# A fused decoder layer on one core: early loads, laid-out bias tiles, separate norm and tanh stages, final scaling on ScalarE

## The chip, the cores and the metric

The kernel runs on one core of a Trainium2 chip. The metric is device time in microseconds of one execution. The texts name the engines TensorE (PE in the rows, PEld its weight loads), VectorE (DVE), ScalarE (ACT), GpSimd (POOL) and SyncE (SP, which only issues transfers here).

## The reference, cut to what matters

One layer (`DEPTH` 1) of a decoder trunk on 512 tokens and 1024 channels, all in float32:

```python
h = rmsnorm(x, norm_mix_g)
proj = h @ w_in                     # mLSTM q,k,v,o,i,f | attention q,k,v | two gates
# branch A: mLSTM, 4 heads x 128: causal conv (width 4) and SiLU on q and k,
#   exponential input gate, sigmoid forget gate, running-max stabiliser
hm = head_rmsnorm(num / max(|den|, exp(-m)), m_norm_g);  ya = (sigmoid(o) * hm) @ w_br_m
# branch B: differential attention, 4 heads, q/k 2 x 64, v 128, causal
a = softmax(q1 k1^T / 8 + bias) - lam * softmax(q2 k2^T / 8 + bias)   # bias: rel_bias[t5_bucket(i - j)]
hd = head_rmsnorm(a @ v, da_norm_g) * (1 - lam_init);  yb = hd @ w_br_d
x = x + (sigmoid(g_a) * ya + sigmoid(g_b) * yb) @ w_out
# FFN: rmsnorm, up (2 x 2816), causal conv (width 3), gelu(gate) * value, down; added to x
x = x + sigmoid(rmsnorm(x) @ w_ple_gate) * (p @ w_ple)
return rmsnorm(x, norm_final_g)
```

## The kernel before, in words

Activations lie with channels on the 128 partitions and 512 tokens along the row, in eight tiles. Each float32 operand of a product is split into a rounded high part (ScalarE, `split`, L89) and the rest (VectorE, L90), and a product is three matmuls: high x high, high x rest, rest x high (`mm3`, L97 to L99). A weight tile of 128x1024 is loaded by SP into `raw` (two buffers), then split into `whi` and `wlo` (two buffers each; `wload`). A projection onto 128 channels is 24 matmuls into one of four PSUM banks of tag `mm`.

The stages: (1) `vproj` for the mLSTM values: eight pairs of an `x` tile and half a weight tile, each pair loaded and split as its buffers come free; squares of `x` are summed for the norm (`rms`). Nine warm matmuls without use run first. (2) The steps of `ORDER`: `if` the scalar gates and their scans (`gates`), `mq`, `mk` conv and SiLU (`conv_silu`), `m` scores and weighted sums of one mLSTM head, `M` its end with norm and output gate, `dq`, `dk`, `dv`, `a`, `A` the same for attention, `ga`, `gb` the branch gates. (3) The merge of the branches, `w_out`, the FFN, and the last part, done in four blocks of 128 tokens, the last of them in halves.

A planner (the tile framework) orders each engine's instructions from the program order as a priority and from its own estimate of times; it also sets all waits. Engines run their queues in order. A tile of a tag waits for a free buffer of the tag; `tc.issue_after` only orders two instructions of one engine, and `tc.high_priority` moves a piece ahead.

The lines of importance: the gate rows are scanned on VectorE (L324, L329), stored to DRAM (`rd`, L332), and each head reads its rows back as a broadcast onto 128 partitions (`rb`, L429), exponentiates (L430), masks (POOL, L431) and multiplies with the scores `s`. The position bias (`make_bias`) is made from a one-hot product on TensorE (`bvp`, L357), stored, broadcast in DRAM and read back with a skew. `rsqrt_of` is a logarithm, an exponential and one Newton step, and loads ScalarE's table with the logarithm ahead (L155); tanh uses another table.

Of the kernel before, what the change touches and what calls it, by code (L numbers as in the profile page):

```python
# [16 lines left out]
P = 128  # L17
# [3 lines left out]
H = 4  # L21
# [16 lines left out]
C_BI = 256  # L38
C_BF = 257
NPAR = 258  # L40
# [10 lines left out]
bias0 if0 mq0 mk0 mq1 mk1 ct0 m0 m1 mk3 mq2 dk0 M0 M1 mk2 m2 mq3 M2 m3 dq0 dv0 M3 a0 dk1 dq1  # L51
A0 a1 A1 dk2 dq2 ga3 dq3 a2 A2 ga0 ga2 gb1 dk3 a3 gb3 gb2 gb0 ga1 A3
# [4 lines left out]
def trunk_kernel(ctx, tc, xT, pT, par, oneh, relb, lamv, w_if, w_in, w_v, w_br, w_out, w_up,  # L57
# [92 lines left out]

    def rsqrt_of(r, v, a, before=None):
# [5 lines left out]
        nc.scalar.activation(r, r, AF.Exp, scale=-0.5, bias=lnb)  # L157
# [23 lines left out]

    ident = cp.tile([P, P], F32, name="ident")
# [16 lines left out]

    def conv_silu(c, scale, name):  # L200
# [3 lines left out]
        nc.gpsimd.memset(u[:, 0:3], 0.0)  # L204
# [13 lines left out]
    def halves(c, name):  # L218

        o = ps("mm", name)  # L220
        proj(o, win(c), 0, h)
        y = tt("ev", "y")
        nc.vector.tensor_mul(y, o, rB)
        return y, (slice(0, 64), slice(64, P))

    def queries(c, name):

        y, rows = halves(c, name)
# [22 lines left out]
    def vw(i, g, kk, old):  # L251

        if old is None:
            raw = wp.tile([P, 1024], F32, tag="raw", name="raw", bufs=2)
            hi = wp.tile([P, 1024], F32R, tag="whi", name="whi", bufs=2)
            lo = wp.tile([P, 1024], F32R, tag="wlo", name="wlo", bufs=2)
            old = (hi, lo, raw)
        hi, lo, raw = old
        c = slice(kk * S, (kk + 1) * S)
        nc.sync.dma_start(raw[:, c], w_v[4 * i + g][:, c])  # L260
        split(hi[:, c], lo[:, c], raw[:, c])
        return old

    def vproj(i, name, first=None):
        os = [ps("mm", f"{name}p{b}") for b in range(NB)]
        xs = []
        for g in range(4):
            w = None if first else wload(w_v[4 * i + g])
            for kk in range(2):
                k = 2 * g + kk  # L270
                if first:
                    x = tt("x", f"x{k}")
                    nc.sync.dma_start(x, xT[:, k, :])
                    h.append(scaled(x, C_GMIX + k, f"h{k}"))
                    w = vw(i, g, kk, w)
                    if k == 1:
                        nc.sync.dma_start(prm[:, KD:], par[:, KD:])
                    xs.append(x)
# [18 lines left out]
    def gates():  # L297
# [3 lines left out]
        with tc.high_priority(offset=180):  # L301
            nc.sync.dma_start(raw, w_if)
# [8 lines left out]
        gi, gf = tt("hn", "gi")[0:H, :], tt("rb", "gf")[0:H, :]  # L311
        for t, c, a in ((gi, C_BI, 0), (gf, C_BF, 32)):
            nc.vector.scalar_tensor_tensor(t, gt[a:a + H, :], prm[a:a + H, c:c + 1], g2[a:a + H, :],
                                           op0=ALU.add, op1=ALU.add)
        e = tt("rb", "ge")[0:H, :]
# [31 lines left out]
    def make_bias():  # L347
        tab = cp.tile([REL_BUCKETS + 1, H], F32, name="tab")
        nc.vector.memset(tab, NEG)
        nc.gpsimd.dma_start(tab[0:REL_BUCKETS, :], relb)  # L350
        bvd = dp.tile([H, 640], F32, name="bvd")
        for i in range(2):
            half = slice(i * 320, (i + 1) * 320)
            oh = tt("hn", "oh", 320)[0:REL_BUCKETS + 1, :]
            nc.gpsimd.dma_start(oh, oneh[:, half])
            o = ps("acc", "bvp", 320)
            nc.tensor.matmul(o[0:H, :], lhsT=tab, rhs=oh, start=True, stop=True)  # L357
            bv = tt("hn", "bv", 320)[0:H, :]
            nc.scalar.activation(bv, o[0:H, :], AF.Copy, scale=8.0)
            nc.gpsimd.dma_start(bvd[:, half], bv)  # L360
        rows = dp.tile([P, H * 640], F32, name="bvrows")
        nc.gpsimd.dma_start(rows, bvd.rearrange("h u -> (h u)").partition_broadcast(P))
        bias = []
        for hh in range(H):
            t = f(rt("bt", f"bias{hh}"))
            src = bass.AP(tensor=rows.tensor, offset=rows[0, hh * 640 + P - 1:hh * 640 + P].offset,
                          ap=[[H * 640 - 1, P], [1, S]])
            nc.gpsimd.dma_start(t, src)
            bias.append(t)
        return bias  # L370
# [36 lines left out]
    def head_norm(o, g, name, extra=None):  # L407

        y = tt("hn", "y")
        nc.scalar.activation(y, o, AF.Copy, scale=col(g))  # L410
        v = tt("hn", "v")
        nc.scalar.activation(v, o, AF.Square)
        ss = ps("sc", name + "ss")
        last = colsum(ss, v)
        if extra is None:
            nc.vector.tensor_scalar(v, ss, 1.0 / P, EPS, op0=ALU.mult, op1=ALU.add)
        else:
            nc.vector.scalar_tensor_tensor(v, ss, 1.0 / P, extra, op0=ALU.mult, op1=ALU.add)
        r = tt("hn", "r")
        rsqrt_of(r, v, ss, last)  # L420
        nc.vector.tensor_mul(y, y, r)
        return y
# [24 lines left out]
    def mlstm_end(hh, num, den, t):  # L447
        em = tt("rb", "em")
# [6 lines left out]
        y = head_norm(num, C_GM + hh, f"hm{hh}", em)  # L455
# [8 lines left out]
    def attention(hh, q, k):  # L464
        av = []
        for i in range(NB):
# [3 lines left out]
            for z in range(2):  # L470
                s = ps("sc", f"ds{hh}{i}{z}", nw)
                for b in range(2):
# [5 lines left out]
                    out=e, in0=s[:, :n], in1=bias[hh][:, S - n:], scale=0.125, scalar=-3.0e38,  # L478
# [17 lines left out]
    def attention_end(hh, o):  # L496
        y = head_norm(o, C_GD + hh, f"hd{hh}")
# [4 lines left out]
    def gate(c, name):  # L502
# [4 lines left out]
        nc.scalar.activation(t, t, AF.Tanh, scale=0.5)  # L507
# [5 lines left out]
    for step in ORDER.split():  # L513
# [13 lines left out]
        elif what == "M":  # L527
            hm[i] = mlstm_end(i, *sums[i], mo.get(i))
        elif what == "dv":
# [322 lines left out]
```

## Time and profile before

| | |
|---|---|
| time, median of 3 runs | 830.45 us (830.2 to 831.01) |
| the profiled execution | 831.68 us; its span 830.0 us |
| TensorE busy | 813.1 us (98%), 3665 matmuls |
| TensorE weight loads | 666.0 us (80%) |
| VectorE / ScalarE / GpSimd busy | 541.2 (65%) / 412.5 (50%) / 28.9 us (3%) |
| HBM traffic over the span | 104 GB/s |

Busy time is the union of an engine's instructions; matmuls overlap their successors, so a busy TensorE isn't one at its peak. An engine's idle time costs something only where TensorE, or the chain to the last output, waits for it.

### The profile page before, as it was taken

The page shows a single profiled execution, that of the slowest core. Times are in us where ns is not written, and L with a number is a line of the kernel's source. Part 1 is how long each engine was busy: PE and PEld are TensorE (multiplying, and loading weights), DVE is VectorE, ACT ScalarE, POOL GpSimd, SP SyncE. Part 2 cuts the span into 40 slices and gives each one's busy share as a digit, 9 for nine tenths or more (in the row PEclk, how much of TensorE's full clock was granted, in tenths as well). Part 3 has the DMA queues.
Part 4 walks back from the last instruction along what each step waited for, and adds up shares of the span by engine and source line. Part 5 has one row for each costly group of instructions (what it writes and reads, how often), then busy time and mean ns, then how long its engine had stood idle before and what let it go on. Part 6 is the DMA issues. An engine that isn't in the chain of part 4 may idle for free.

```text
span 830.0 us, 9910 instructions
## 1 busy us (share of the span) xinstructions
PE 813.1 (98%) x3665; PEld 666.0 (80%) x3665; DVE 541.2 (65%) x875; ACT 412.5 (50%) x624; POOL 28.9 (3%) x117
## 2 busy tenths in 40 slices
PE   9999999999999999999999999999999999999995
PEld 7777778887878888888788888888888888888884
DVE  7698787699767854456677777777777343343546
ACT  7556877687776433234654444444444432232433
POOL 0111100000000000000000000000000000000000
PEclk9999999999999999999999999999999999999998
DMA  6472333222122233352333222333223323333402
GB/s 223 136 207 96 102 109 109 78 77 71 58 76 77 77 102 102 123 181 92 111 103 102 101 82 97 102 108 120 87 92 101 96 89 99 94 112 96 142 36 77
DMA packets 28425, 85.97 MB, mean 104 GB/s; under 512 B 3462, under 2 KB 5146, under 8 KB 28248
## 3 DMA queue, kind: packets, MB, share of 16 engines
q1 hardware_dynamic: 27256, 81.96, 30.9%
q0 software_dynamic: 832, 3.11, 1.3%
q8 instruction: 29, 0.48, 0.2%
q10 hardware_dynamic: 288, 0.27, 0.1%
q14 instruction: 20, 0.16, 0.1%
HBM read 83.19 MB, written 3.45 MB: 104 GB/s over the span
## 4 chain that ended last, share of the span: by engine, by line
PE 85%; ACT 5%; DMA 4%; DVE 4%; issue 1%; POOL 0%; SPq 0%; POOLq 0%; DVEq 0%; ACTq 0%
PE uv L99 5%; PE wd L98 5%; PE wd L99 5%; PE uv L97 5%; PE uv L98 5%; PE wd L97 5%; PE ug L99 5%; PE ug L97 5%; PE ug L98 5%; PE gb L98 2%; PE gb L97 2%; PE gb L99 2%; PE ga L97 2%; PE ga L99 2%; PE ga L98 2%; PE wo L97 2%
## 5 line engine op out<-in xcount | busy, mean ns | idle before, releaser
L89 ACT CAST whi<-raw 128x1024 fp32r<-128x1024 f32 (+1 forms) x137 | 138.3, 1010 | 206.4 <-issue 73.0
L90 DVE TENSOR_TENSOR wlo<-raw,whi 128x1024 fp32r<-128x1024 f32 (+1 forms) x136 | 159.8, 1176 | 87.2 <-ACT whi L89 85.8
L97 PE MATMUL wd<-gh,whi 128*128 128x512 f32 x176 | 68.5, 389 | 0.0
L98 PE MATMUL wd<-gl,whi 128*128 128x512 f32 x176 | 68.5, 389 | 0.0
L99 PE MATMUL wd<-gh,wlo 128*128 128x512 f32 x176 | 68.5, 389 | 0.0
L588 DVE SCALAR_TENSOR_TENSOR y<-u,prm,y 128x512 f32<-128x512 f32 x88 | 65.6, 749 | 1.5
L89 ACT CAST gh<-y 128x512 fp32r<-128x512 f32 x22 | 13.7, 621 | 55.5 <-DVE y L597 55.5
L583 DVE TENSOR_TENSOR u<-uv,rffn 128x512 f32<-128x512 f32 x22 | 15.2, 692 | 38.2 <-PE uv L99 38.2
L97 PEld LDWEIGHTS wd<-gh,whi 128*128 128x128 f32 x176 | 33.0, 188 | 6.9
L98 PEld LDWEIGHTS wd<-gl,whi 128*128 128x128 f32 x176 | 33.0, 188 | 6.9
L99 PEld LDWEIGHTS wd<-gh,wlo 128*128 128x128 f32 x176 | 33.0, 188 | 6.8
L586 ACT ACTIVATE y<-u,prm 128x512 f32<-128x512 f32 x44 | 35.7, 814 | 0.2
L595 ACT ACTIVATE y<-y 128x512 f32<-128x512 f32 x22 | 13.9, 632 | 38.9 <-DVE y L588 38.9
L97 PE MATMUL wo<-mxh,whi 128*128 128x512 f32 x64 | 24.9, 389 | 0.0
L98 PE MATMUL wo<-mxl,whi 128*128 128x512 f32 x64 | 24.9, 389 | 0.0
L99 PE MATMUL wo<-mxh,wlo 128*128 128x512 f32 x64 | 24.9, 389 | 0.0
L90 DVE TENSOR_TENSOR gl<-y,gh 128x512 fp32r<-128x512 f32 x22 | 15.2, 692 | 14.7 <-ACT gh L89 14.7
L481 ACT ACTIVATE e<-e,mx 128x128 f32<-128x128 f32 (+3 forms) x32 | 17.8, 558 | 7.0 <-DVE mx L480 6.8
L210 DVE SCALAR_TENSOR_TENSOR y<-u,prm,y 128x512 f32<-128x512 f32 x24 | 17.8, 743 | 2.1 <-ACT y L208 2.0
L582 POOL MEMSET u<- 128x2 f32 x44 | 4.3, 99 | 366.6 <-DVE y L588 357.2
L571 DVE TENSOR_TENSOR x<-x,wo 128x512 f32<-128x512 f32 x8 | 5.5, 687 | 17.2 <-PE wo L99 17.2
L477 DVE CUSTOM_DVE_ANT_0 e<-ds,bias 128x128 f32<-128x128 f32 (+3 forms) x32 | 15.1, 482 | 2.3 <-PE ds L473 2.2
(1093 smaller groups left out, 2226.7 us busy)
## 6 DMA issues: line engine op xcount, KB each, us to landing
raw<-in_w_up SPq DMA_DIRECT2D x44, 512.0 KB, 3.3
raw<-in_w_in SPq DMA_DIRECT2D x36, 512.0 KB, 3.4
raw<-in_w_down SPq DMA_DIRECT2D x16, 512.0 KB, 3.6
x<-in_xT SPq DMA_DIRECT2D x16, 256.0 KB, 4.5
raw<-in_w_br SPq DMA_DIRECT2D x8, 512.0 KB, 3.2
raw<-in_w_out SPq DMA_DIRECT2D x8, 512.0 KB, 3.8
raw<-in_w_gate SPq DMA_DIRECT2D x8, 512.0 KB, 3.4
raw<-in_w_down SPq DMA_DIRECT2D x8, 384.0 KB, 3.3
```

What stands on the lines that cost most here:

```text
L89: nc.scalar.copy(hi, src)
L90: nc.vector.tensor_sub(lo, src, f(hi))
L97: nc.tensor.matmul(o, lhsT=lh, rhs=rh, start=start, stop=False)
L98: nc.tensor.matmul(o, lhsT=lh, rhs=rl, start=False, stop=False)
L99: nc.tensor.matmul(o, lhsT=ll, rhs=rh, start=False, stop=stop)
L210: nc.vector.scalar_tensor_tensor(y, u[:, i:i + S], col(c0 + i), y, op0=ALU.mult, op1=ALU.add)
L477: nc.vector.tensor_tensor_reduce(out=e, in0=s[:, :n], in1=bias[hh][:, S - n:], scale=0.125, scalar=-3.0e38, op0=ALU.add, op1=ALU.max, accu ...
L481: nc.scalar.activation(e, e, AF.Exp, bias=mx[:, 1:2], accum_out=mx[:, 2:3])
L583: nc.vector.tensor_mul(u[:, 2:514], o, rB)
L586: nc.scalar.activation(y, u[:, 2:514], AF.Identity, scale=col(c0 + 2), bias=col(c0 + 3))
L588: nc.vector.scalar_tensor_tensor(y, u[:, i:i + S], col(c0 + i), y, op0=ALU.mult, op1=ALU.add)
L595: nc.scalar.activation(gt, gt, AF.Gelu_apprx_tanh)
```

## The change

- The eight `x` tiles and the eight weight halves of the first stage are all issued on SP at the start, the halves into buffers of tag `hz` in place of `raw`; the other parameters follow, and the load for `if` behind them. The first half of `whi` is copied on VectorE.
- The position bias comes as four tiles laid out beforehand, loaded by POOL, at a later step (`bias0` behind `mk2`), behind the last `memset` traced up to there. The factor 1/8 moves from the softmax's reduction to the queries.
- The scalar gates add their biases in one instruction of 36 rows in place of two of 4 rows.
- `M` ends with the product of gate and numerator and with the mean square; the rest of the norm and the split are steps `N` of their own, behind the first attention head and later. Only head 0 of the attention loads the logarithm's table ahead.
- The tanh of the branch gates are issued behind the last exponential of the attention norms, in the merge loop.
- In the last part the product with the final gain comes ahead of the norm, and the scaling by the norm is on ScalarE for the first three blocks; the last block's halves are multiplied first, then finished with priority.

```diff
-bias0 if0 mq0 mk0 mq1 mk1 ct0 m0 m1 mk3 mq2 dk0 M0 M1 mk2 m2 mq3 M2 m3 dq0 dv0 M3 a0 dk1 dq1
-A0 a1 A1 dk2 dq2 ga3 dq3 a2 A2 ga0 ga2 gb1 dk3 a3 gb3 gb2 gb0 ga1 A3
+if0 mq0 mk0 mq1 mk1 ct0 m0 m1 mk3 mq2 dk0 M0 M1 mk2 bias0 m2 mq3 M2 m3 dq0 dv0 M3 a0 dk1 dq1
+A0 a1 N0 A1 dk2 dq2 N1 ga3 dq3 a2 N2 A2 ga0 ga2 gb1 dk3 N3 a3 gb3 gb2 gb0 ga1 A3
...
+    for k in range(KD):
+        xs.append(tt("x", f"x{k}"))
+        nc.sync.dma_start(xs[k], xT[:, k, :])
+        raws.append(f(rt("hz", f"raw{k}")))
+        nc.sync.dma_start(raws[k], w_v[k // 2][:, k % 2 * S:(k % 2 + 1) * S])
+    fed = nc.sync.dma_start(prm[:, KD:], par[:, KD:])
...
+        if g + kk == 0:
+            nc.vector.tensor_copy(hi[:, c], raw)
+            nc.vector.tensor_sub(lo[:, c], raw, f(hi[:, c]))
+        else:
+            split(hi[:, c], lo[:, c], raw)
...
+        nc.vector.scalar_tensor_tensor(g2[0:36, :], gt[0:36, :], prm[0:36, C_B:C_B + 1], g2[0:36, :],
+                                       op0=ALU.add, op1=ALU.add)
+        gi, gf = g2[0:H, :], g2[32:32 + H, :]
...
     def make_bias():
...
+            with tc.issue_after(last_pool.ins):
+                nc.gpsimd.dma_start(t, biasT[:, hh * S:(hh + 1) * S])
...
     def mlstm_end(hh, num, den, t):
...
+        y, v = f(rt("hz", f"hmy{hh}")), f(rt("hz", f"hmv{hh}"))
+        nc.scalar.activation(y, num, AF.Copy, scale=col(C_GM + hh))
+        ss, _ = mean_square(num, v, f"hm{hh}")
+        nc.vector.scalar_tensor_tensor(v, ss, 1.0 / P, em, op0=ALU.mult, op1=ALU.add)
...
+        return y, v
+
+    def mlstm_norm(hh, y, v):
+        r, t = tt("hn", "r"), tt("hn", "t")
+        rsqrt_of(r, v, t)
+        nc.vector.tensor_mul(t, y, r)
         hi, lo = rt("hz", f"hmh{hh}"), rt("hz", f"hml{hh}")
-        split(hi, lo, y, 0.5)
+        split(hi, lo, t, 0.5)
...
+        rsqrt_of(r, v, ss, None if hh else last)
...
-        nc.scalar.activation(t, t, AF.Tanh, scale=0.5)
         return t
...
+        with tc.issue_after(last_exp.ins):
+            for t in (ta, tb):
+                nc.scalar.activation(t, t, AF.Tanh, scale=0.5)
...
         for n in range(2):
-            x = x3[b, n]
-            nc.vector.scalar_tensor_tensor(x, x, r, gB[n], op0=ALU.mult, op1=ALU.mult)
-            nc.sync.dma_start(out[b][:, n * S:(n + 1) * S], x)
+            nc.scalar.activation(x3[b, n], x3[b, n], AF.Copy, scale=r)
+            nc.sync.dma_start(out[b][:, n * S:(n + 1) * S], x3[b, n])
...
+        nc.vector.tensor_scalar_mul(x[:, :half], x[:, :half], r)
+        nc.vector.scalar_tensor_tensor(x[:, half:], x[:, half:], r, gB[1][:, half:], op0=ALU.mult, op1=ALU.mult)
         nc.sync.dma_start(out[b][:, S:], x)
...
+        nc.scalar.activation(x3[b, 0], x3[b, 0], AF.Copy, scale=r)
+        nc.scalar.dma_start(out[b][:, :S], x3[b, 0])
...
+        with tc.high_priority():
+            x = embed(b, S, half, os[0], xt[:, :half], 1)
+            nc.vector.tensor_scalar(ss[b][:, 3:4], ss[b][:, 0:1], ss[b][:, 1:2], D * EPS, op0=ALU.add, op1=ALU.add)
+            embed(b, S + half, half, os[1], xt[:, half:], 2)
+        nc.vector.tensor_mul(x, x, gB[1][:, :half])
```

## Rows read from the trace of the kernel before

**Rows 1.** Waits of TensorE: engine, line, waited for: us in total, times, longest.
```profile
PE num L97 <- ACT pph L89: 2.5, 4, 1.4
PE s L97 <- ACT mk0h L92: 2.0, 1, 2.0
```

**Rows 2.** By stretches: length, busy us of each engine, granted clock, DMA share, GB/s.
```profile
62.00:160.00 98.00, 94.30 (x433) 76.74 (x434) 75.54 (x118) 71.78 (x116) 8.59 (x31) 0.98 0.32 100
160.00:280.00 120.00, 119.70 (x566) 96.09 (x566) 97.32 (x254) 87.50 (x165) 3.67 (x15) 1.00 0.22 71
```

**Rows 3.** Timeline of the head: start, us, engine, line, operation, out<-in, count, idle before.
```profile
1.52 4.21 PE L126 MATMUL warm<-idle 128*128 128x512 f32 x9 [1.52 <-DVE idle L123]
...
4.32 0.72 ACT L139 ACTIVATE h0h<-x,prm 128x512 fp32r<-128x512 f32 x1 [1.79 <-DMA prm<-in_par]
...
5.07 0.75 DVE L140 SCALAR_TENSOR_TENSOR h0l<-x,prm,h0h 128x512 fp32r<-128x512 f32 x1 [3.19 <-ACT h0h L139]
...
5.46 0.60 ACT L89 CAST whi<-raw 128x512 fp32r<-128x512 f32 x1
...
6.12 0.50 PE L97 MATMUL mvp<-whi,h0h 128*128 128x512 f32 x1 [0.39 <-ACT whi L89]
```

**Rows 4.** Timeline of TensorE around the first bias product.
```profile
29.16 0.40 PE L99 MATMUL mvp<-whi,h7l 128*128 128x512 f32 x1
29.49 0.70 PE L357 MATMUL bvp<-oh,tab 33*4 33x320 f32 x2
30.12 0.50 PE L307 MATMUL if<-h0h,whi 128*128 128x512 f32 x1
```

**Rows 5.** Timeline of VectorE behind the gate matmuls.
```profile
36.30 0.28 DVE L377 TENSOR_TENSOR lvp<-lv 128x128 f32<-128x128 f32 x1
...
38.20 0.14 DVE L383 TENSOR_TENSOR nlam<-lexp 128x1 f32<-128x1 f32 x1
38.37 0.74 DVE L313 SCALAR_TENSOR_TENSOR gf<-gt,prm,g 4x512 f32<-4x512 f32 x1
```

**Rows 6.** Chain of waits, 40 to 63 us: start, us, what.
```profile
49.48 3.00 DMA rd<-rows
...
62.87 0.50 PE s L97
```

**Rows 7.** By stretches, granted clock third from the end.
```profile
63.60:67.10 3.50, 3.50 (x10) 2.92 (x10) 3.50 (x6) 0.62 (x1) 0.10 (x1) 0.51 0.00 0
87.00:89.00 2.00, 0.72 (x4) 0.26 (x2) 0.76 (x2) 1.62 (x5) 0.29 (x1) 1.00 0.71 109
```

**Rows 8.** Table loads of ScalarE: groups of 60 to 300 us, and timeline at 91.
```profile
L155 ACT ACT_TABLE_LOAD x8 | 10.3, 1283 | 0.1
...
L507 ACT ACT_TABLE_LOAD x4 | 5.1, 1283 | 0.1
...
91.74 1.28 ACT L155 ACT_TABLE_LOAD   x1
93.03 0.64 ACT L450 ACTIVATE em<-em 128x512 f32<-128x512 f32 x1
```

**Rows 9.** A norm's step on VectorE by line; the last softmax by stretches.
```profile
L159 DVE SCALAR_TENSOR_TENSOR hm0ss<-v,hm0ss x1: 689/689/689, 104.6 to 104.6; 128x512 f32<-128x512 f32 x1
...
250.00:260.00 10.00, 10.00 (x50) 8.28 (x49) 9.98 (x38) 8.08 (x19) 0.00 (x0) 1.00 0.33 104
260.00:270.00 10.00, 10.00 (x50) 8.07 (x49) 4.57 (x9) 5.54 (x11) 0.35 (x2) 1.00 0.15 53
```

**Rows 10.** Timeline of the end.
```profile
820.40 0.47 ACT L710 ACTIVATE pg<-pgs,rple 128x256 f32<-128x256 f32 x1 [2.28 <-PE pgs L99]
820.86 0.42 DVE L712 SCALAR_TENSOR_TENSOR pg<-pg,pw 128x256 f32<-128x256 f32 x1
...
822.85 0.41 DVE L716 TENSOR_TENSOR x<-pg,xt 128x256 f32<-128x256 f32 x1
...
823.83 0.43 DVE L769 TENSOR_TENSOR x<-x,gfin 128x256 f32<-128x256 f32 x1 [0.57 <-ACT pg L717]
824.17 0.21 DVE L732 TENSOR_SCALAR v<-ss 128x1 f32<-128x1 f32 x1
...
825.60 0.51 ACT L738 ACTIVATE x<-x,rf 128x256 f32<-128x256 f32 x1 [1.80 <-DVE rf L662]
...
826.44 0.35 ACTq L740 DMA_DIRECT2D out<-x  x1
```

More of the change, by code (lines that the diff above doesn't have):

```diff
@@ L37 @@
 C_FCONV = 80
-C_BI = 256
-C_BF = 257
-NPAR = 258
+C_B = 256
+NPAR = 257
 ROW_OFF = [0, 512, 896, 1152, 1280]
@@ L156, in rsqrt_of @@
         nc.scalar.activation(r, v, AF.Ln, scale=2.0 ** -LN_SHIFT)
-        nc.scalar.activation(r, r, AF.Exp, scale=-0.5, bias=lnb)
+        nonlocal last_exp
+        last_exp = nc.scalar.activation(r, r, AF.Exp, scale=-0.5, bias=lnb)
         nc.scalar.activation(a, r, AF.Square)
@@ L198, in win @@
         return wload(w_in[c])
+    last_pool = None
     def conv_silu(c, scale, name):
@@ L216, in conv_silu, with halves @@
         return hi, lo
-    def halves(c, name):
+    def halves(c, name, scale=1.0):
         o = ps("mm", name)
@@ L222, in halves @@
         y = tt("ev", "y")
-        nc.vector.tensor_mul(y, o, rB)
+        nc.vector.scalar_tensor_tensor(y, o, scale, rB, op0=ALU.mult, op1=ALU.mult)
         return y, (slice(0, 64), slice(64, P))
     def queries(c, name):
-        y, rows = halves(c, name)
+        y, rows = halves(c, name, 0.125)
         qs = []
@@ L249, in keys, with vw @@
         return ks
-    def vw(i, g, kk, old):
+    def vw(g, kk, old):
         if old is None:
-            raw = wp.tile([P, 1024], F32, tag="raw", name="raw", bufs=2)
             hi = wp.tile([P, 1024], F32R, tag="whi", name="whi", bufs=2)
             lo = wp.tile([P, 1024], F32R, tag="wlo", name="wlo", bufs=2)
-            old = (hi, lo, raw)
-        hi, lo, raw = old
+            old = (hi, lo)
+        hi, lo = old
         c = slice(kk * S, (kk + 1) * S)
-        nc.sync.dma_start(raw[:, c], w_v[4 * i + g][:, c])
-        split(hi[:, c], lo[:, c], raw[:, c])
+        raw = raws[2 * g + kk]
+        if g + kk == 0:
[3 more added lines that the diff above has]
+            split(hi[:, c], lo[:, c], raw)
         return old
@@ L301, in gates @@
         with tc.high_priority(offset=180):
-            nc.sync.dma_start(raw, w_if)
+            with tc.issue_after(fed.ins):
+                nc.sync.dma_start(raw, w_if)
             split(w[:, :, 0:64], w[:, :, 64:P], raw.rearrange("p (k c) -> p k c", c=64))
@@ L347, in make_bias @@
     def make_bias():
[L348 to L363, printed above, removed]
+        out = []
         for hh in range(H):
             t = f(rt("bt", f"bias{hh}"))
[L366 to L370, printed above, removed]
+            with tc.issue_after(last_pool.ins):
+                nc.gpsimd.dma_start(t, biasT[:, hh * S:(hh + 1) * S])
+            out.append(t)
+        return out
     def make_nlam():
@@ L405, in weighted, with mean_square @@
             nc.tensor.matmul(o, lhsT=ones, rhs=pl, start=False, stop=j == NB - 1)
[L407 to L411, printed above, removed]
+    def mean_square(o, v, name):
         nc.scalar.activation(v, o, AF.Square)
         ss = ps("sc", name + "ss")
[L414 to L422, printed above, removed]
+        return ss, colsum(ss, v)
     def mlstm(hh):
@@ L477, in attention @@
                 nc.vector.tensor_tensor_reduce(
-                    out=e, in0=s[:, :n], in1=bias[hh][:, S - n:], scale=0.125, scalar=-3.0e38,
+                    out=e, in0=s[:, :n], in1=bias[hh][:, S - n:], scale=1.0, scalar=-3.0e38,
                     op0=ALU.add, op1=ALU.max, accum_out=mx[:, 0:1])
@@ L496, in attention_end @@
     def attention_end(hh, o):
-        y = head_norm(o, C_GD + hh, f"hd{hh}")
+        y, v, r = tt("hn", "y"), tt("hn", "v"), tt("hn", "r")
+        nc.scalar.activation(y, o, AF.Copy, scale=col(C_GD + hh))
+        ss, last = mean_square(o, v, f"hd{hh}")
+        nc.vector.tensor_scalar(v, ss, 1.0 / P, EPS, op0=ALU.mult, op1=ALU.add)
+        rsqrt_of(r, v, ss, None if hh else last)
+        nc.vector.tensor_mul(y, y, r)
         hi, lo = rt("hz", f"hdh{hh}"), rt("hz", f"hdl{hh}")
@@ L528, in trunk_kernel @@
             hm[i] = mlstm_end(i, *sums[i], mo.get(i))
+        elif what == "N":
+            hm[i] = mlstm_norm(i, *hm[i])
         elif what == "dv":
@@ L796, in _bucket_onehot @@
     b = np.where(n < exact, n, np.minimum(large, REL_BUCKETS - 1))
-    b = np.where(u <= 511, b, REL_BUCKETS)
-    return (b[None, :] == np.arange(REL_BUCKETS + 1)[:, None]).astype(np.float32)
+    t = np.concatenate([rel_bias, np.full((1, H), NEG, np.float32)])[np.where(future, REL_BUCKETS, b)]
+    return t.transpose(0, 2, 1).reshape(P, H * S)
 def _pack(x, p, rel_bias, norm_mix_g, w_in, b_if, m_conv_w, m_conv_b, m_norm_g, da_lambda, da_norm_g,
```

67 lines of the change are left out of this document (26 added, 41 removed).

## The prediction, made before the changed kernel was built or run

> **What bounds the kernel now.** I read the page first: its engine line gives TensorE 813.1 of 830.0 us, the other engines 65% at most (both stand in the small table). So an edit pays only where it removes TensorE work, closes a gap in TensorE, or shortens the ends where TensorE doesn't work. The waits of TensorE come next: the gaps are few, the longest single one 2.0 us before the first score matmul of the mLSTM (`s`), which waits for ScalarE's `mk0h`, and four of 2.5 us together before `num` [rows 1]. The view by stretches says where: the mLSTM stage (62 to 160 us) has 98 − 94.30 = 3.7 us without TensorE work, the attention stage (160 to 280) only 0.3 [rows 2]. The timelines of the two ends and of the places that the diff touches give the terms. The profiled execution took 831.68 us, 1.68 more than its span; the median of the runs shown is 830.45, 1.23 less. I sum against 831.68 and subtract 1.23 at the end.
>
> **Head.** The first projection matmul starts at 6.12 us, behind `h0h` (ScalarE, from 4.32), `acc` and then `whi`, the last to come; the warm matmuls keep TensorE busy until 1.52 + 4.21 = 5.73 [rows 3]. The change gives the first half of `whi` to VectorE, which is idle then, so ScalarE's queue no longer stands in the way. `h0h` still waits for the parameter load that ScalarE issues first, which the change leaves alone. Then the warm matmuls end last: 6.12 − 5.73 = 0.4 saved. Bounds: 0.6 saved (they overlap their successor) and 0.4 lost, where VectorE takes the 0.75 us `h0l` ahead of the copy. I take −0.4. That the sixteen loads go out without waiting for the `raw` buffers gives nothing to TensorE here: of its few waits [rows 1] only the first, for `whi`, lies in this stage. The load of the remaining parameters moves behind them; its first reader is beyond 34 us.
>
> **Position bias.** Two matmul groups `bvp` go: TensorE spends 30.12 − 29.49 = 0.63 us on the first, the second repeats it at 34 us [rows 4]. Together −1.26. Nothing hides them, since the projections stand right behind. The bound is half of that: the first pair may have covered the wait of `if` for a free PSUM bank. The four loads of laid-out bias and the five-step chain through DRAM leave POOL's queue at this place; four loads come back behind `mk2`, and the `lamv` load with them. The masks of head 2 can stand behind the five issues in POOL's queue; POOL is busy only 8.59 of 98 us in that stage [rows 2], so it has the time. I take 0; if the cover is gone, a mask is late by what five issues take.
>
> **The wait at 60.5 us.** From the gate matmuls a chain leads over VectorE's scans, a store to DRAM and the broadcast back to ScalarE's `rb`, behind which `mk0h` stands in ScalarE's queue. The change takes from VectorE in this stretch `lvp` and `lsum` (0.28 each), one of two gate additions (0.74) and two small `nlam` steps (0.15 each): 1.6 us [rows 5]. VectorE is the one that sets the pace here, so the chain is 1.6 us shorter, while TensorE arrives 0.63 us earlier (the second `bvp` lies between). The wait becomes 2.02 − 1.6 + 0.63 = 1.05, a gain of 0.97. More may come: the store of `rows` takes 3.00 us there, beside the bias transfers that go [rows 6]. After the wait TensorE's granted clock was 0.51 for 3.5 us, its lower level of 1.2 GHz, which costs 3.5 × 0.49 = 1.7; after a stretch with 0.72 us of work in 2 us it stayed at 1.00 [rows 7]. So with a wait of about 1 us I also count the 1.7 as saved: −2.7 in all. Bounds: −3.7 (all of it) and +2 (the written order of TensorE is made anew by the planner, and a wait as long as this one may appear elsewhere).
>
> **mLSTM and attention.** Tanh and the logarithm sit in different tables. In the stage from 60 to 300 us the two lines with most of the loads have 12, of 1.283 us [rows 8]. With the norms moved behind the first attention head and the gates' tanh behind the last exponential, two are left, so at least 10 × 1.283 = 12.8 us leave ScalarE. Of the norms, per head, a logarithm, an exponential, a square and a split move from the mLSTM to the attention stage on ScalarE; on VectorE four instructions of about 0.69 us (one is shown), 2.8 us per head, 11 us in all [rows 9]. So the mLSTM stage gets easier, where ScalarE was busy 71.78 of 98 us, and VectorE rises from 97.3 to 108 of 120 us in the attention stage. `s` starts at 62.87 [rows 6], so 0.87 of the 3.7 us of the mLSTM stage belong to the wait before it, and 2.8 remain; all name ScalarE [rows 1]. I take −0.5 for both stages; bounds −2.8 and the 11 us of VectorE. At the merge of the branches, the sixteen tanh and one table load stand on ScalarE while TensorE still has the products of the other heads; ScalarE is busy 5.54 of 10 us there [rows 9]: 0. Without that cover it is the load and the first two tanh, some 2.7 us by the rows of `h0h` and of the loads.
> Weighed against the trace: behind a table load at 91.74 the next ScalarE instruction starts at 93.03, 1.29 us later [rows 8]. The Trainium skill (ScalarE: Activation LUTs, section "What ACT_TABLE_LOAD costs") gives 1.28 for the load and 1.38 more for a drain, 2.66 for each switch. By the page the same ten loads would free 27 us of ScalarE; the trace shows no such drain, and as ScalarE isn't what the end waits for, the sum would move by no more than the bound above.
>
> **Tail.** After the last matmul ScalarE's tanh starts at 820.40, but VectorE, held by two scalings of the block before that wait for its norm and by a product with the final gain, reaches the last half's addition only at 822.85 [rows 10]. The change puts block 2's scaling on ScalarE and the gain products ahead, so nothing ahead of the multiply on VectorE waits for the norm any more, and I count it free at 820.5. Then the tanh (0.47) ends at 820.87, the multiply takes 0.42, so the addition starts at 821.3. From there to the scale took 825.60 − 822.85 = 2.75, of which 0.34 is the gain product in front of `v`; 2.41 remain: scale at 823.7. ScalarE's half is now 512 wide; the nearest row of that kind, `h0h`, took 0.72: 824.4, and a little for the issue: 824.6 instead of 826.44, −1.8. Bounds −2.0 and 0 (the two new ScalarE scalings, waiting for POOL's power, stand ahead of the tanh in its queue).
>
> **Sum.** −0.4 − 1.3 − 2.7 − 0.5 − 1.8 = −6.7: 831.68 − 6.7 = 825.0, less 1.23: 823.8 us.
>
> **Rivals.**
> A. The wait before `s` stays. The planner that orders TensorE places `s` where it believes `mk0h` ready, and a chain that it also believes shorter is answered by an earlier `s`. For it: the order was made from planned times, and the chip missed them here by the 2.0 us of [rows 1]. Against it: the transfers of the chain get lighter, which a plan need not see. Then 2.7 is missing: 831.68 − 4.0 − 1.23 = 826.5.
> B. The emptier ScalarE closes the mLSTM stage altogether, and the wait at 60 us goes whole: 1.0 and 2.3 more, 820.5. For it: the waits of [rows 1] for `num` and `s` name ScalarE. Against it: `rb`, which ScalarE works on ahead of them, still comes by DRAM.
> C. Slower: VectorE becomes the bound in the attention stage. It is busy 9.98 of 10 us in the softmax of the last head, with 4.57 of 10 right after [rows 9]; the 11 us of norm work fit only if they fall into the light stretches. VectorE works in order, so a norm that stands ahead of a head's softmax holds all its scores, and TensorE, once the gate projections are used up, waits. Price 2.8 us for each head, 11.2 with all four: 831.68 − 6.2 + 11.2 − 1.23 = 835.5. It decides from 6.2 us on, where it has eaten the other terms, that is from the third head. Against it: 22.7 us of VectorE are free in the stage, and eight gate projections of 24 matmuls each are there to fill.
> D. The new order doesn't do what it says: table loads are put back between logarithm and tanh, as the planner may bring a norm forward. They cost ScalarE 1.283 each and TensorE little; the time is that of the forecast without the 0.5: 824.3, within its own range.
>
> **How the numbers follow.** Forecast with D 0.47, A 0.25, B 0.16, C 0.12. The likeliest gives 823.8, its own range 821.5 to 825.5. For 8 in 10 the range goes down to 819.5 (B, with both ends at their bounds) and up to 830, which takes in A with the head and the first `bvp` unpaid, and the beginning of C. What the measurement can tell apart is about 0.2%, 1.7 us: faster means under 828.8, slower over 832.1. The forecast and B are faster, A but for 0.02 at its upper end; of C two thirds end slower, the rest within. Faster 0.86, same 0.06, slower 0.08.
>
> **What would show it.** Right: first projection matmul at about 5.7; no `bvp`; the first `s` waits 1 us or less and the granted clock stays at 1.00 after it; two table loads from 60 to 300 us; VectorE at 90% from 160 to 280 us with TensorE gaps there under 1 us; last output issue 4.2 us after the last tanh starts, not 826.44 − 820.40 = 6.0. Wrong: a granted clock of 0.5 anywhere after the start, TensorE waiting in the attention stage for VectorE's `mx`, or a tanh of the last block held in ScalarE's queue.

## The result, and the profile after

The changed kernel is slower: median 835.84 us (835.26 to 836.90, 4 runs) beside 830.73 (830.20 to 831.17, 4 runs) of the kernel before on the same chip, ratio 1.0057 [1.0037, 1.0078]. The profiled execution took 836.26 us, its span 833.3.

To see where the time went, I cut the span at four events of TensorE that both kernels have. (In after, `hd2ss` and other steps are reordered, so a landmark inside a stage can mislead; between these four TensorE has the same matmuls in both kernels, but for the four of `bvp`.) The forecast gave its −0.5 to the mLSTM and the attention stage together; it stands in the mLSTM's row here.

| stretch of TensorE, us | before | after | difference | forecast |
|---|---|---|---|---|
| start to last `mvp` (head) | 29.56 | 29.88 | +0.32 | −0.4 |
| last `mvp` to first `ds` (gates, mLSTM) | 135.74 | 129.96 | −5.78 | −4.5 (`bvp` −1.26, wait −2.7, stage −0.5) |
| first `ds` to last `yb` (attention, merge) | 191.91 | 200.68 | +8.77 | 0 |
| last `yb` to last `pgs` (`w_out`, FFN) | 463.10 | 463.06 | −0.04 | 0 |
| last `pgs` to the end (tail) | 9.66 | 9.70 | +0.04 | −1.8 |

The differences add up to 3.3 us, that of the two spans, while the medians lie 5.1 apart. The profiled execution after took 2.96 us outside its span, the one before 1.68: that is 1.3 of the other 1.8, for which no stage accounts.

TensorE's waits after (engine, line, waited for: us in total, times, longest):

```profile
PE yb L96 <- ACT hdh L91: 6.5, 1, 6.5
...
PE s L96 <- ACT mk0h L91: 1.4, 1, 1.4
PE num L96 <- ACT pph L88: 1.1, 2, 0.6
```

`s` and `num` wait less than in [rows 1]; a new wait of 6.5 us is longer than all of those. It stands at the merge of the branches, where the products of the last attention head, `hd3`, are due. The stretches (columns as in [rows 2], the last one lies around the end of the wait):

```profile
62.00:160.00 98.00, 96.90 (x455) 79.44 (x454) 71.14 (x113) 57.72 (x98) 11.50 (x35) 1.00 0.35 116
160.00:280.00 120.00, 113.89 (x539) 90.29 (x537) 100.39 (x260) 82.24 (x166) 3.72 (x15) 0.99 0.19 66
277.84:284.67 6.83, 4.00 (x9) 2.81 (x10) 4.58 (x7) 5.39 (x9) 0.00 (x0) 0.50 0.00 0
```

In the mLSTM stage 98 − 96.90 = 1.1 us are without TensorE work instead of 3.7; in the attention stage 6.1 instead of 0.3. Around the end of the wait TensorE's granted clock is 0.50, its level of 1.2 GHz, for 6.83 us, as it was for some 3.5 us behind the wait at 60 us in the kernel before [rows 7]; there it now stays at 1.00.

What holds `hdh`: ScalarE's timeline at the merge, after.

```profile
273.80 0.72 ACT L159 ACTIVATE r<-r,lnb 128x512 f32<-128x512 f32 x1
274.54 1.28 ACT L555 ACT_TABLE_LOAD   x1
275.84 0.63 ACT L555 ACTIVATE ga<-ga 128x512 f32<-128x512 f32 x1
276.37 0.58 ACT L160 ACTIVATE hd3ss<-r 128x512 f32<-128x512 f32 x1
...
279.49 0.61 ACT L555 ACTIVATE ga<-ga 128x512 f32<-128x512 f32 x1
280.01 0.61 ACT L91 ACTIVATE hdh<-y 128x512 fp32r<-128x512 f32 x1
```

And VectorE's, after:

```profile
276.50 0.69 DVE L560 SCALAR_TENSOR_TENSOR ga<-ga,ya 128x512 f32<-128x512 f32 x1 [3.40 <-ACT ga L555]
277.10 0.69 DVE L161 SCALAR_TENSOR_TENSOR hd3ss<-v,hd3ss 128x512 f32<-128x512 f32 x1
277.83 0.69 DVE L162 SCALAR_TENSOR_TENSOR r<-hd3ss,r 128x512 f32<-128x512 f32 x1
```

The same place before, ScalarE:

```profile
272.94 0.72 ACT L157 ACTIVATE r<-r,lnb 128x512 f32<-128x512 f32 x1
273.69 0.60 ACT L158 ACTIVATE hd3ss<-r 128x512 f32<-128x512 f32 x1
276.51 0.63 ACT L92 ACTIVATE hdh<-y 128x512 fp32r<-128x512 f32 x1 [2.21 <-DVE y L421]
```

From the last exponential to the split `hdh` it took 276.51 − 272.94 = 3.57 us before and 280.01 − 273.80 = 6.21 after: the table load and a tanh stand ahead of the square that the norm needs, more tanh ahead of the split, and VectorE's product `ga` waits 3.40 us for its tanh with the norm's steps queued behind it. That is 2.6 us of the 6.5. The rest is that the last head comes late: TensorE was 5.45 us ahead at the first `ds`, yet its `hd3ss` (the sum of squares for the last head's norm) ends at 272.37 instead of 271.11.

The head after, ScalarE:

```profile
4.79 0.72 ACT L138 ACTIVATE h0h<-x,prm 128x512 fp32r<-128x512 f32 x1 [2.26 <-DMA prm<-in_par]
```

VectorE:

```profile
5.54 0.75 DVE L139 SCALAR_TENSOR_TENSOR h0l<-x,prm,h0h 128x512 fp32r<-128x512 f32 x1 [3.58 <-ACT h0h L138]
6.21 0.42 DVE L275 CAST whi<-raw 128x512 fp32r<-128x512 f32 x1
```

`h0l` does stand ahead of the copy, and `h0h`, which waits for the parameters, starts 0.47 us later than in [rows 3] (over all runs it starts between 4.20 and 5.25); the first `mvp` starts at 6.78 instead of 6.12. From there on TensorE waits for nothing in this stage.

The tail after, ScalarE, VectorE and the last issue:

```profile
823.62 1.32 ACT L730 ACTIVATE x<-x,rf 128x512 f32<-128x512 f32 x2
824.84 0.45 ACT L714 ACTIVATE pg<-pgs,rple 128x256 f32<-128x256 f32 x1
...
825.78 0.42 DVE L720 TENSOR_TENSOR x<-pg,xt 128x256 f32<-128x256 f32 x1
...
828.15 0.72 ACT L739 ACTIVATE x<-x,rf 128x512 f32<-128x512 f32 x1 [1.41 <-DVE rf L666]
828.90 0.38 ACTq L740 DMA_DIRECT2D out<-x  x1
```

From the start of the last tanh to the last issue it is 828.90 − 824.84 = 4.1 us, as forecast, instead of 6.0 [rows 10]. But the two scalings of block 2 stand ahead of that tanh, and it starts 1.26 us behind the last matmul's end (823.58) instead of 0.09. From the last issue to the end of the span it takes 4.4 us instead of 3.5. These two, 1.2 and 0.8, use up the gain of 2.0; the forecast counted on neither. No run was made for the second.

### The profile page after: what moved, and what is told of

The parts are those of the page before. It is cut to its first block, busy times and chain, and to the rows that moved or that the text cites. A ratio compares the mean times of both kernels' runs of the same rounds, so it can differ in the third digit from the quotient of the medians.

```text
span 833.3 us, 9859 instructions
## 1 busy us (share of the span) xinstructions
PE 811.2 (97%) x3661; PEld 665.4 (80%) x3661; DVE 539.7 (65%) x873; ACT 397.8 (48%) x614; POOL 27.3 (3%) x111
## 4 chain that ended last, share of the span: by engine, by line
PE 81%; ACT 2%; issue 1%; DVE 1%; POOL 0%; POOLq 0%; DVEq 0%; ACTq 0%
PE uv L96 5%; PE wd L98 5%; PE wd L96 5%; PE uv L98 5%; PE uv L97 5%; PE wd L97 5%; PE ug L96 5%; PE ug L98 5%; PE ug L97 5%; PE ga L96 2%; PE ga L98 2%; PE ga L97 2%; PE gb L98 2%; PE gb L97 2%; PE gb L96 2%; PE wo L96 2%
## 5 line engine op out<-in xcount | busy, mean ns | idle before, releaser
L89 DVE TENSOR_TENSOR wlo<-raw,whi 128x1024 fp32r<-128x1024 f32 (+2 forms) x135 | 159.3, 1180 | 89.5 <-ACT whi L88 88.1
L96 PE MATMUL yb<-hdh,whi 128*128 128x512 f32 x32 | 13.2, 412 | 6.5 <-ACT hdh L91 6.5
```

What stands on the lines that cost most here:

```text
L89: nc.vector.tensor_sub(lo, src, f(hi))
L96: nc.tensor.matmul(o, lhsT=lh, rhs=rh, start=start, stop=False)
```

## The experiments

Each compares with the kernel before on its own chip. Two theories of the attention stretch's 8.8 us: **T**, the deferred tanh of the gates (table load and tanh in front of the last norm); **N**, the norms that moved from the mLSTM into the attention stage (rival C of the prediction; in the expectations of e13 and e14, C and E are two forms of N). "Stage" below is the time from the first `ds` to the last `yb`.

**e1_tanh_back.** The gates' tanh back in `gate()`, and every attention norm loads its table ahead again.
```diff
         nc.vector.tensor_mul(t, o, rB)
+        nc.scalar.activation(t, t, AF.Tanh, scale=0.5)
         return t
...
-        rsqrt_of(r, v, ss, None if hh else last)
+        rsqrt_of(r, v, ss, last)
```


> The changed kernel with one part undone: the tanh of each branch gate stands behind its projection again (each attention norm loads the logarithm's table ahead, as before). Theory T (the tanh that were moved to the merge make the new TensorE gap of 6.5 us before `yb` and the half clock behind it, some 8.9 us together): the gap falls under 1 us, the granted clock stays at 1.00 there, and the time is about 835.8 - 8.5 = 827.3 us, though ScalarE loads its tables some nine times more between 160 and 300 us. Rival N (the norms in the attention stage use up the gate projections early and make VectorE late, so that TensorE runs dry whatever ScalarE does): the gap stays over 4 us, time 833 to 836.

835.32 us, ratio 1.0045 [1.0030, 1.0060]; stage 199.0, the wait of `yb` 3.2 us instead of 6.5 and no low clock behind it, but two new waits in the attention stage (`at` for VectorE's `e` 1.2, `ds` for `mx` 0.6). The wait lies between the two expectations, the time is N's; T alone falls.

**e2_norm_back.** The four norms directly behind each `M` again, no `N` steps; the tanh stays deferred.
```diff
-            hm[i] = mlstm_end(i, *sums[i], mo.get(i))
+            hm[i] = mlstm_norm(i, *mlstm_end(i, *sums[i], mo.get(i)))
```


> The changed kernel with the other part undone: the mLSTM norm and its split follow each head's end directly, and there are no norm steps in the attention stage; the gates' tanh stay at the merge. Theory T: the gap before the last head's products stays at 5 us or more with half clock behind it, and the mLSTM stage gets its table loads and some 3 us of TensorE gaps back: 835 to 839 us. Rival N: the gap falls under 2 us; with the 3 us of the mLSTM stage given back the time is 828 to 831.

831.82 us, ratio 1.0008 [0.9999, 1.0017]; stage 194.5 with 1.6 us of `ds` waiting for `mx` in it, no wait at the merge. The stretch from the last `mvp` to the first `ds` is 132.9 instead of 130.0: parting the norms from `M` had gained 3 us there. N accounts for most of the stage's loss; the time is 0.8 us above N's range.

**e3_tanh_after_split.** The tanh stay deferred, but behind ScalarE's split of the last head instead of its exponential.
```diff
-        split(hi, lo, y, 1.0 - LAM_INIT)
+        last_exp = nc.scalar.activation(hi, y, AF.Copy, scale=1.0 - LAM_INIT)
+        nc.vector.scalar_tensor_tensor(lo, y, 1.0 - LAM_INIT, f(hi), op0=ALU.mult, op1=ALU.subtract)
```


> The changed kernel, the gates' tanh still at the merge but behind ScalarE's split of the last attention head in place of behind its exponential. This parts theory T in two. Tq (the table load and the tanh stand in ScalarE's queue ahead of the square and the split of that head): the split comes some 2.6 us earlier, the gap falls from 6.5 to about 3.9 us, time about 831 to 833. Tp (without a tanh no product `ya` leaves its PSUM bank, so TensorE has nothing else to do): what then remains of the gap, some 4 us, is its share. If Tq were all, the gap would be under 1 us and the time 827; if Tp were all, 835 to 836.

834.12 us, ratio 1.0033 [1.0021, 1.0046]; stage 198.4, the wait 3.9 us. So the queue at the merge is 6.5 − 3.9 = 2.6 us of the wait, as the timelines said, and 2.3 us of the stage; 3.9 stay. The time is above the 831 to 833 that was expected; the profiled execution was the fastest of its ten, 832.13.

**e4_block2_vector.** Block 2's final scaling on VectorE.
```diff
+            if b == NB - 2:
+                nc.vector.tensor_scalar_mul(x3[b, n], x3[b, n], r)
+            else:
+                nc.scalar.activation(x3[b, n], x3[b, n], AF.Copy, scale=r)
```


> The changed kernel, with the norm scaling of block 2 (the last but one) on VectorE as a plain product with a column in place of ScalarE. Theory Q (two scalings of 0.7 us stand in ScalarE's queue ahead of the last tanh, which starts 1.26 us after its matmuls ended): the last tanh starts within 0.1 us of the last matmul, the last output is issued 1.2 us earlier, time 834.6. Rival V (VectorE holds the last half anyway, its scalings only change places): no gain, the last tanh is early but the addition behind it is late, 835.8.

837.01 us, ratio 1.0059 [1.0041, 1.0077], no gain; from the last `pgs` to the end 9.33 instead of 9.70. VectorE holds the chain now:

```profile
826.68 0.87 DVE L731 TENSOR_SCALAR x<-x,rf 128x512 f32<-128x512 f32 x2
827.47 0.42 DVE L774 TENSOR_TENSOR x<-x,gfin 128x256 f32<-128x256 f32 x1
827.80 0.42 DVE L716 SCALAR_TENSOR_TENSOR pg<-pg,pw 128x256 f32<-128x256 f32 x1
```
The last tanh ended at 826.96; the multiply starts at 827.80, behind the two scalings.

**e11_tail.** Block 2's two scalings on ScalarE, but behind the last square, where ScalarE waits for the norm of the last block anyway.
```diff
+        with tc.issue_after(last_sq.ins):
+            scale_out(b - 1, r2)
```


> Only the place of block 2's two ScalarE scalings in ScalarE's queue is changed: behind the last square in place of ahead of the last tanh. Theory: these two (1.32 us, waiting for the power from POOL) made the last tanh 1.24 us late; from the last gate matmul to the end 8.3 to 8.6 us instead of 9.70, time 834.4 to 834.8. Rival: the chain is then held by VectorE (gain products ahead of the last multiply) or by the later output of block 2: 9.2 or more, no gain that can be measured.

834.76 us, ratio 1.0041 [1.0028, 1.0053]; from the last `pgs` to the end 8.55 us. ScalarE:

```profile
825.43 0.47 ACT L715 ACTIVATE pg<-pgs,rple 128x256 f32<-128x256 f32 x1
826.86 0.42 ACT L723 ACTIVATE pg<-x 128x256 f32<-128x256 f32 x1 [0.96 <-DVE x L721]
...
827.28 1.32 ACT L734 ACTIVATE x<-x,rf 128x512 f32<-128x512 f32 x2
828.78 0.72 ACT L743 ACTIVATE x<-x,rf 128x512 f32<-128x512 f32 x1 [0.18 <-DVE rf L666]
```
The tanh starts 0.10 us behind the last matmul (825.33), and the 1.32 us lie beside VectorE's norm. The 1.15 us of the tail agree with the theory; the ratio alone would not tell it apart.

**e5_head_order.** VectorE copies `whi` ahead of `h0l`.
```diff
+                    if k == 0:
+                        w = vw(g, kk, w)
+                        with tc.issue_after(copied.ins):
+                            h.append(scaled(x, C_GMIX + k, f"h{k}"))
```


> Only the order on VectorE at the start is changed: the copy of the first half of whi stands ahead of h0l. Theory: in the changed kernel the first projection matmul moved from 6.12 to 6.78 us because VectorE did h0l (5.54) before the copy (6.21); with the copy first it starts at 5.6 to 6.0 us, and the whole kernel is 0.7 to 1.0 us faster than the changed one: 834.8 to 835.1. Rival: the stage is held by the arrival of the later x tiles and weight halves (the last mvp was only 0.32 us later than before, not 0.66), so the first matmul comes earlier but the last mvp doesn't, and the time stays within 0.3 of 835.84.

835.61 us, ratio 1.0050 [1.0037, 1.0063]. TensorE, end of the warm matmuls and start of the projection:

```profile
1.52 4.21 PE L125 MATMUL warm<-idle 128*128 128x512 f32 x9 [1.52 <-DVE idle L122]
5.86 1.88 PE L96 MATMUL mvp<-whi,h0h 128*128 128x512 f32 x4
```
The first matmul comes 0.92 us earlier, as the theory said, but the last `mvp` ends at 29.67, only 0.21 earlier. The rival is right on the time and not on its cause: behind the first `mvp` TensorE waits for no `x` tile and no weight here either. What takes 0.72 of the 0.92 back is that the first four matmuls run in 1.88 us here and in 1.16 in after; the last section shows why.

**e6_both_back.** The edits of e1 and e2 together.

> Norms directly behind M again and the gates' tanh back in their steps, all other parts of the change kept. Theory NT (the norms in the attention stage cost, the deferred tanh adds a queue part): no wait over 2 us at the merge, granted clock not lowered there, mLSTM gains only some 2.5 us at its last dvp as without the N steps; 829.5 to 831.5, within 0.2% of the kernel before. Rival O (another part of the change, the late bias loads or the 0.125 on the queries, costs several us): 833 or more.

834.07 us, ratio 1.0032 [1.0019, 1.0044]: a miss, and slower than e2. Stage 196.6, with a wait of 2.0 for `hdh` and one of 1.6 for `mx`. ScalarE at the last norm:

```profile
269.21 1.28 ACT L156 ACT_TABLE_LOAD   x1
270.50 1.28 ACT L507 ACT_TABLE_LOAD   x1
271.79 0.63 ACT L507 ACTIVATE ga<-ga 128x512 f32<-128x512 f32 x1
272.44 1.28 ACT L157 ACT_TABLE_LOAD   x1
273.74 0.63 ACT L157 ACTIVATE r<-v 128x512 f32<-128x512 f32 x1
274.38 1.28 ACT L159 ACT_TABLE_LOAD   x1
```
The planner put a gate's tanh between the table load and the logarithm it was meant for, so the last norm has four loads around it, where the kernel before had one ahead of its logarithm (270.93). So what e6 loses against e2 isn't rival O but rival D of the prediction, brought by undoing the edit, and at 2.1 us of the stage it isn't "little" for TensorE as D said. The wait for `mx` stands in e2 too. Rival O, several us by another part of the change, is bounded by e8 below, which keeps the late bias loads and the scaled queries and has a stage only 0.9 us longer than before.

**e8_norm_early.** The four `N` steps directly behind `M3`, ahead of the attention; the tanh stays deferred. The edit also loads the logarithm's table ahead for head 0's norm (so do e12, e14 and e15).
```diff
-... dq0 dv0 M3 a0 dk1 dq1 A0 a1 N0 A1 dk2 dq2 N1 ga3 dq3 a2 N2 A2 ga0 ga2 gb1 dk3 N3 a3 ...
+... dq0 dv0 M3 N0 N1 N2 N3 a0 dk1 dq1 A0 a1 A1 dk2 dq2 ga3 dq3 a2 A2 ga0 ga2 gb1 dk3 a3 ...
```


> The four N steps are moved from the attention stage to directly behind M3, where VectorE was busy only 1.57 of 10 us (140 to 150 us) and 5.52 (150 to 160); the tanh of the gates stays deferred. Theory N (the 8.7 us lost from the last dvp to the last yb come mostly from the norms' 11 us of VectorE and their ScalarE steps between the attention heads): the gain of the mLSTM stage (-5.4 at its last dvp) stays to within 1.5 us and the loss to the last yb falls to about that of the kernel with the norms put back (+2.6): 829 to 831, faster than or equal to before. Theory T (the deferred tanh alone makes the gap): the wait of yb for hdh stays over 5 us, 834 to 836. Rival L (the work is only shifted: VectorE and ScalarE now hold up dvp and the first attention head): last dvp -2 or worse, 832 to 835.

828.91 us, ratio 0.9966 [0.9953, 0.9978]: faster than the changed kernel and the one before. The stage is 192.8 us, the mLSTM stretch 130.4, and no wait for `hdh` is left. The stretch that took the norms up, in the changed kernel (columns as in [rows 2]):

```profile
140.00:160.00 20.00, 20.00 (x91) 16.57 (x90) 7.09 (x9) 5.96 (x8) 0.00 (x0) 1.00 0.29 105
```
and with the norms there:
```profile
140.00:160.00 20.00, 20.00 (x90) 16.57 (x89) 16.53 (x23) 17.45 (x25) 0.00 (x0) 1.00 0.25 83
```
VectorE (third engine) has 9.4 us more in these 20 and TensorE still works all the time. Measured from the first `ds`, heads 0 to 3 reach the sum of squares of their norm (the end of `hd0ss` to `hd3ss`) at 23.3, 50.1, 76.5 and 105.3 us, in the changed kernel at 22.3, 49.8, 84.1 and 112.5: the whole delay is there at head 2, and the fourth norm adds none to it.

**e13_norms_together.** The `N` steps stay in the attention stage, all four directly behind `a1`.
```diff
-A0 a1 N0 A1 dk2 dq2 N1 ga3 dq3 a2 N2 A2 ga0 ga2 gb1 dk3 N3 a3
+A0 a1 N0 N1 N2 N3 A1 dk2 dq2 ga3 dq3 a2 A2 ga0 ga2 gb1 dk3 a3
```

> All four N steps stay in the attention stage but directly behind the first head (with the written order N0 N1 N2 N3 behind a1), none later. Theory C (it is the sum of VectorE's and ScalarE's work of this stage that counts, wherever in it the norms stand): heads 2 and 3 are late as in the changed kernel, the wait of yb for hdh stays at 4 us or more, 834 to 836. Rival E (only the late ones, N2 and N3, stand in the way of the last heads' chain): hd2ss and hd3ss come within 1 us of where they were with the norms directly behind M3, no wait over 2 us at the merge, 829 to 831.

834.71 us, ratio 1.0034 [1.0021, 1.0046]; stage 199.3. Theory C is right on the price, not on the place: heads 2 and 3 are late (85.3 and 111.1 us behind the first `ds`, so rival E falls), but `yb` waits only 0.3 us for `hdh`; TensorE's loss comes earlier, where VectorE's split of a weight tile is held.

```profile
PE ga L98 <- DVE wlo L89: 3.4, 1, 3.4
```

**e14_n3_late.** `N0` to `N2` behind `M3`, `N3` alone ahead of `a3`.
```diff
-... M3 N0 N1 N2 N3 a0 ... gb1 dk3 a3 ...
+... M3 N0 N1 N2 a0 ... gb1 dk3 N3 a3 ...
```

> N0, N1 and N2 directly behind M3, N3 alone where the change has it, between attention heads 2 and 3. Theory C: a quarter of the work comes back to the stage and costs a quarter of what four cost or nothing, since VectorE has some 8 of 40 us free from 200 to 240: 829 to 830.5. Rival E (one norm ahead of the last head is what delays it): the wait of yb for hdh is 3 us or more, 832 to 835.

831.77 us, ratio 1.0004 [0.9995, 1.0014]; stage 195.3, so one norm costs 2.5 us, between the two expectations, with a wait of 1.2 for `hdh`. It shows how. VectorE in the last head's softmax with all norms early (e8):

```profile
247.44 0.34 DVE L483 TENSOR_SCALAR e<-e,mx,nlam 128x128 f32<-128x128 f32 x1
247.75 0.42 DVE L475 CUSTOM_DVE_ANT_0 e<-ds,bias 128x256 f32<-128x256 f32 x1
```
and with `N3` late:
```profile
247.17 0.68 DVE L161 SCALAR_TENSOR_TENSOR t<-hmv,t 128x512 f32<-128x512 f32 x1
247.91 0.67 DVE L162 SCALAR_TENSOR_TENSOR r<-t,r 128x512 f32<-128x512 f32 x1
...
248.75 0.68 DVE L456 TENSOR_TENSOR t<-hmy,r 128x512 f32<-128x512 f32 x1
...
249.62 0.41 DVE L475 CUSTOM_DVE_ANT_0 e<-ds,bias 128x256 f32<-128x256 f32 x1
...
250.44 0.69 DVE L92 SCALAR_TENSOR_TENSOR hml<-t,hmh 128x512 fp32r<-128x512 f32 x1
```
ScalarE in the same run:
```profile
249.47 0.63 ACT L91 ACTIVATE hmh<-t 128x512 fp32r<-128x512 f32 x1 [2.15 <-DVE t L456]
```
The norm's four instructions stand in the middle of the softmax; the scores' next tile is read at 249.62 instead of 247.75, and behind it everything up to `hdh` is late. ScalarE, to which the norm brings work too, idles 2.15 us for VectorE there, so it isn't ScalarE that holds the head at this place. From the first `ds` to the end of `hd3ss` it takes 108.2 us instead of 105.3, 2.8 more; the four instructions take 2.7.

**e15_early_tanh_back.** e8 with the gates' tanh back in their steps.

> Norms directly behind M3 and the gates' tanh back in their steps, so that the attention norms load the logarithm's table again (18 table loads in all instead of 10). Theory: with the norms out of the attention stage deferring the tanh isn't a loss but a gain, since each norm's chain is shorter by its load; putting it back costs 1.5 to 3 us against the same kernel with the tanh deferred, 830.5 to 832 with a wait of 1 to 2 us of yb for hdh. Rival T (the deferred tanh in ScalarE's queue at the merge costs by itself): 1 to 3 us faster than with the tanh deferred, 826 to 828.

831.11 us, ratio 0.9989 [0.9979, 0.9999]; stage 194.9, with a wait of 2.0 for `hdh` and the same four table loads around the last norm. As expected by the theory.

**e12_best.** e8, e11 and e5 together.

> Three edits of the earlier runs together: norms directly behind M3, block 2's scalings behind the last square, the first whi copy ahead of h0l. Theory: they lie at three places and add up: the norms' place gave some 6.5 us against the changed kernel, the tail 1.1, the head 0 to 0.6; so 0.4 to 0.6% under the kernel before (some 827 us where before is 831). Rival: what is saved at the head or tail is covered anyway, then as with the norms alone (ratio 0.9966 or above).

826.30 us (825.72 to 826.87), ratio 0.9933 [0.9921, 0.9946]. Stage 192.8 and tail 8.55: these two keep what they gave alone, and the span is 824.5 instead of 833.3. The last `mvp` at 29.79 is where after has it (29.88); a gain from the head isn't shown.

## Why the prediction was wrong

The measured time lies above the whole range. The stage times side by side (first `ds` to last `yb`, us; 191.9 before):

| norms | tanh deferred | tanh in its step |
|---|---|---|
| behind each `M` | 194.5 (e2) | 196.6 (e6) |
| all behind `M3` | 192.8 (e8) | 194.9 (e15) |
| among the attention heads | 200.7 (after) | 199.0 (e1) |

**The step that failed** is the attention half of "I take −0.5 for both stages". The norms among the heads cost 200.7 − 192.8 = 7.9 us against the same norms behind `M3`. I had put their 11 us at the upper bound and at rival C, which I gave 0.12. What misled me was to set 11 us of work against 22.7 us of free VectorE time in the stage. VectorE rose only from 97.3 to 100.4 of 120 us, 84% and not the 90% that was to show the forecast right; over the stage it was never full. The price comes from order: a norm that is queued in a softmax makes that head late, in e14 by 2.8 us for 2.7 us of instructions; VectorE's free time lies elsewhere (before, it was busy 9.98 of 10 us in the last softmax and 4.57 right behind it [rows 9]). TensorE, ahead by 5.45 us and with its gate projections used up earlier (the first `yb` at 263.6 instead of 272.3), meets the late last head at the merge.

C's mechanism is what came, and one head's price: 2.8 us each, 2.5 of the stage measured. Four cost 7.9 and not C's 11.2, and 2.3 of the 7.9 are the tanh in the queue of the late head (e3). That C's sum, 835.5, lies beside the measured 835.84 is luck: it counts gains at the head and the tail that didn't come, and four full norms. Of the signs named for being wrong, two came: a granted clock of 0.50, at the merge, and the last tanh held in ScalarE's queue.

**Merge tanh, 0.** Its condition, "while TensorE still has the products of the other heads", failed with the late head, and the price named for lost cover, 2.7, is what e3 took away: 2.6 us of the wait. With the norms out of the way the deferral is a gain of 2 us in either place (first two rows of the table). At least a part of that is the planner's order: where the tanh went back, four loads stand around the last norm and `yb` waits 2.0 us behind them (e6, e15). The kernel before, with its tanh in its step and one load at this norm, has a stage of 191.9, shorter than all in the table. The Trainium skill (ScalarE: Activation LUTs, section "Table sets: the hidden batching unit") asks to batch activations by table set; here the batch paid 2.0 us (e8 against e15), and lost 1.7 (after against e1) where the late norms had made ScalarE's queue at the merge critical. Its drain of 1.38 us with every switch (the Trainium skill, ScalarE: Activation LUTs, section "What ACT_TABLE_LOAD costs") is not seen in e6 either: the loads at 269.21 and 270.50, of 1.28 us, follow each other within 0.01 us.

**mLSTM, −0.5.** Too small: the stretch from the last `mvp` to the first `ds` gained 5.78 where −4.5 was forecast, and 2.95 of it belong to parting the norms from `M` (e2 keeps 2.83 without it). That is a little past the bound of −2.8; `num` and `s` together now wait 2.5 us instead of 4.5.

**`bvp` and the wait at 60.5 us.** The start of the first `if` moves by 0.74 us against that of the matmul before it, the first `mq` by 0.72: −1.46, forecast −1.26. The wait before `s` went from 2.0 to 1.4, not to 1.05, and the low clock behind it is gone. In e2, with the norms back behind each `M`, the stretch gains 2.83, 1.1 less than the forecast −3.96; its `M` still differs from the one before, so the two terms can't be read off it alone.

**Head, −0.4.** The case named as its bound occurred: `h0l` ahead of the copy, and `h0h` itself was later. e5 undoes the order, but its last `mvp` gains only 0.21. The term left out how fast the first matmuls run: from the first `mvp` to the end of the last it takes between 23.1 and 25.2 us in these profiles, and the +0.32 can't be told from that.

**Tail, −1.8.** The chain from the last tanh got shorter by 2.0 us as worked out, and the case named as the bound of 0 occurred, the two scalings ahead of the tanh. e11 puts 1.15 back, so 1.1 us are gained on the kernel before; the other 0.8 of the 2.0 lie behind the last issue, which the forecast took for the end.

## What to carry to other kernels

Free time of an engine summed over a stage does not say that work fits in there: look whether the moved instructions land inside a chain that runs on that engine in order, and price them there at their full length first (here one norm of 2.7 us cost 2.5, four of 11 cost 7.9). Look instead for a stretch where no such chain runs (here VectorE's 13 free us of 20 while TensorE does projections). When an edit names its own bad case ("stand ahead of the tanh in its queue"), read the written order for it before giving it a small weight.

## What the runs showed of the hardware that was not expected

At the start the first projection matmuls run at different speeds from one profile to the next. In after:

```profile
6.78 1.16 PE L96 MATMUL mvp<-whi,h0h 128*128 128x512 f32 x4 [1.44 <-DVE whi L275]
7.78 0.39 PE L97 MATMUL mvp<-wlo,h0h 128*128 128x512 f32 x1
```
In e4:
```profile
7.24 2.04 PE L96 MATMUL mvp<-whi,h0h 128*128 128x512 f32 x4 [1.51 <-ACT h1h L138]
9.09 0.63 PE L97 MATMUL mvp<-wlo,h0h 128*128 128x512 f32 x1
```
0.63 us is what a matmul of this shape takes at the merge in after where the granted clock is 0.50, so here it is the lower level too. The trace agrees: its record of the granted clock has no entry before 11.06 us in e4 and 4.77 us in after, and reads 1.0 from there (the view by stretches prints 1.00 also where the record has none); in e4 the matmuls are at 0.39 us from 11.15 on. The last `mvp` ends at 32.12 in e4 and at 29.88 in after: some 2 us that come and go between executions, and perhaps a part of the spread of 1 to 4 us in the times of one kernel. e1, e8, e11, e14 and e15 too were profiled with a late rise (10.0 to 10.9 us, last `mvp` between 31.1 and 31.9); in e5, e12 and e13 it comes at 7.4 to 7.7 and in the others by 6.2 (last `mvp` from 29.3 to 30.0 in all of these). Stage times, not ends, are therefore compared above. What decides was not tried; the idle time between the warm matmuls and the first `mvp` alone does not, with 1.44 us in after and 0.55 in e11, which rises at 10.0.

Nor does the length of a wait alone decide whether the clock falls behind it: it fell to 0.50 behind 2.0 us before `s` in the kernel before, behind 3.4 us in e13 and behind 6.5 in after, and stayed at 1.00 behind 3.2 us at the merge in e1 and 2.0 in e6.
